# The first token tile and its gains in column halves, and all bias lines ahead of the second tile's transposes

## The chip, the cores and the metric

The kernel runs on one core of a Trainium2 chip. What counts is the time of one execution on the device in microseconds; the kernel before takes 1675.51 us (median of 3 runs, 1674.7 to 1675.98).

## The reference

One layer of a bidirectional encoder, on a prompt of 256 tokens and a sample of 1024 tokens, 1024 wide, all in float32. What matters here is its beginning:

```python
def _rmsnorm(x, g):
    x32 = x.astype(jnp.float32)
    y = x32 * lax.rsqrt(jnp.mean(x32 * x32, axis=-1, keepdims=True) + RMS_EPS)
    return (y * g.astype(jnp.float32)).astype(x.dtype)
...
    h = _rmsnorm(x, g_mix)
    z = h @ w_in
...
    rel = np.arange(3 * n)[None, :] - n - np.arange(n)[:, None]
    bias = bias_table.astype(jnp.float32)[_rel_bucket(rel * dist_scale)]
```

Tokens are normalized and scaled by the gains g, and projected to queries, keys, values and gates. Two branches of banded attention follow (one with a sink, one dilated in three groups), both with a bias that depends only on the distance of query and key, looked up in a table of 32 buckets. The branches are gated, merged and projected; an MLP with a squared ReLU and a last normalization end the layer.

## The kernel before

The 1280 tokens are ten tiles of 128 rows. A float32 product is made of three products of a high and a low part (`hi`, `lo`): ScalarE rounds to `hi`, VectorE subtracts to get `lo`, TensorE multiplies hi*hi, hi*lo and lo*hi. The order of the work in this first part is the order in which the code is written: each engine runs its instructions in that order.

The part around the change is the start (lines 689 to 908). SyncE issues the loads in program order: the first token tile (`load_x(0)`, line 702, 512 KB), the gains g spread over 128 partitions (line 831, 512 KB), the second token tile, the first half of a table `hot` (line 740, 132 KB), the first quarter of the value weights (`load_v`, line 709, 512 KB), the second half of `hot`, the other quarters, and then further token tiles and the rest. A DMA issue also waits for the landing of the DMA that stands eight before it, as they share eight semaphores in turn. The transfer of the bucket table `tab` (line 734, 2.5 KB) goes through ScalarE's queue.

Meanwhile TensorE runs `warm(15)`: 15 matmuls of the identity, whose result nobody uses (two records each in the trace). Then come the token tiles:

- `square(t)`: ScalarE squares the tile with an accumulator along the row (line 757) and takes the root of mean + eps (line 759).
- `scale(t)`: VectorE takes the reciprocal (line 763) and multiplies the tile by it and by g in one instruction (line 764), into `xn`.
- `turn(t)` is a generator of three steps: TensorE transposes `xn` in eight blocks of 128 columns into two banks of PSUM, four to a bank (line 336); ScalarE evicts four high parts (line 790) and VectorE four low parts (line 792); at last ScalarE copies plain parts for later use.
- `draw(j)`: one of four matmuls that turn the bucket table into the bias lines of all heads (line 744); j 0 and 1 read the first half of `hot`, 2 and 3 the second. All four sum into one bank, and `store_lines` reads it only during the fourth token tile.
- `split_v(0, i)`: the value weights' high part on ScalarE and low part on VectorE or GpSimd (lines 720 and 721).
- `values(t, v, ps)`: the value projection, three matmuls for each of eight blocks (line 819).

TensorE's order is: warm matmuls, transposes of tile 0, draws 0 and 1, transposes of tile 1, draws 2 and 3, value matmuls of tiles 0 and 1. ScalarE and VectorE square and scale tile 1 ahead of evicting the transposes of tile 0.

Of the kernel before, what the change touches and what calls it, by code (L numbers as in the profile page):

```python
# [10 lines left out]
F32 = mybir.dt.float32  # L11
F32R = mybir.dt.float32r
AF = mybir.ActivationFunctionType
ALU = mybir.AluOpType

P = 128
D = 1024
# [9 lines left out]
EPS = 1e-6  # L27
# [70 lines left out]
def encoder_kernel(  # L98
# [5 lines left out]
    nc = tc.nc  # L104
    PSUM = bass.MemoryType.PSUM

    def x_rows(t):
        return x_sample[0, P * t : P * (t + 1), :] if t < 8 else x_prompt[0, P * (t - 8) : P * (t - 7), :]
# [13 lines left out]
    small = ctx.enter_context(tc.tile_pool(name="small", bufs=4))  # L122
# [4 lines left out]
    def slot(name, shape=(P, D), dt=F32):  # L127
        return slots.tile(list(shape), dt, name=name, tag="m", bufs=N_M)
# [7 lines left out]
    def bank(tag, name=None):  # L136
        return psum.tile([P, 512], F32, name=name or tag, tag=tag, bufs={"mm": 3, "sc": 2, "pt": 2, "pv": 1}[tag])
# [120 lines left out]
    def copy(out, in_, scale=None):  # L258
        flip[0] ^= 1
        if flip[0]:  # L260
            nc.scalar.activation(out, in_, AF.Copy, scale=1.0 if scale is None else scale)
        elif scale is None:
            nc.vector.tensor_copy(out, in_)
        else:
            nc.vector.tensor_scalar(out, in_, scale, None, op0=ALU.mult)
# [41 lines left out]
    hp, xn = {}, {}  # L307
# [381 lines left out]
    with ExitStack() as pre:  # L689
# [5 lines left out]
        xs, sds = {}, {}  # L695
        gm = slot("gm")
        NV = (512, 384)
        v_raw, v_parts = {}, {}

        def load_x(t):  # L700
            xs[t] = slot("xt")
            nc.sync.dma_start(xs[t], x_rows(t))

        def load_v(v, i):

            raw = v_raw[v, i] = slot("vraw", (P, 2, NV[v]))
            ks = slice(2 * i, 2 * i + 2)
            if v == 0:
                nc.sync.dma_start(raw, w_in3[:, ks, OFF_V : OFF_V + 512])
            else:  # L710
                nc.sync.dma_start(raw[:, :, :P], w_in3[:, ks, 640 : 640 + P])
                nc.sync.dma_start(raw[:, :, P:], w_in3[:, ks, OFF_V + 512 : OFF_V + 768])

        def split_v(v, i, eng=nc.vector):
            if v == 0:
                hi, lo = wslot("vhi", (P, 2, 512), F32R), wslot("vlo", (P, 2, 512), F32R)
            else:
                hi, lo = own("v2", (P, 2, 384), F32R, 8), own("v2", (P, 2, 384), F32R, 8)
            src = v_raw.pop((v, i))
            nc.scalar.activation(hi, src, AF.Copy)  # L720
            eng.tensor_tensor(lo, src, hi.bitcast(F32), op=ALU.subtract)
            v_parts[v, i] = hi, lo

        def warm(n):
            ps = bank("mm", "warm")
            for _ in range(n):
                nc.tensor.matmul(ps[:, :P], ident, ident, start=True, stop=True, skip_group_check=True)

        pads = NL // 512
# [8 lines left out]
        def load_hot(i):  # L738
            hots.append(slot("hot")[: BUCKETS + 1, :])
            nc.sync.dma_start(hots[i], hot[:, D * i : D * i + D])  # L740

        def draw(j):

            nc.tensor.matmul(drawn, tab[:, edge - 32 * j : edge - 32 * j + P],
                             hots[j // 2][:, 512 * (j % 2) : 512 * (j % 2) + 512], start=not j, stop=j == pads - 1)
# [8 lines left out]
        def square(t):  # L754
            xn[t] = slot("xn")
            ss = small.tile([P, 1], F32, name="ss")
            nc.scalar.activation(xn[t], xs[t], AF.Square, accum_out=ss)
            sds[t] = small.tile([P, 1], F32, name="sd")
            nc.scalar.activation(sds[t], ss, AF.Sqrt, bias=eps, scale=1.0 / D)

        def scale(t):
            rs = small.tile([P, 1], F32, name="rs")
            nc.vector.reciprocal(rs, sds.pop(t))
            nc.vector.scalar_tensor_tensor(xn[t], xs.pop(t), rs, gm, op0=ALU.mult, op1=ALU.mult)

        def two(name):
            return [slot(name, (P, 2, 512)) for _ in range(2)]
# [53 lines left out]
        def evac(t, v, ps):  # L821
# [6 lines left out]
            nc.gpsimd.dma_start(scr_v[rows, 512 * v : 512 * v + NV[v]], vo)  # L828

        load_x(0)  # L830
        nc.sync.dma_start(gm, g_mix[0].partition_broadcast(P))
        load_x(1)
        load_hot(0)
        load_v(0, 0)
        load_hot(1)
        for i in range(1, 4):
            load_v(0, i)
        for t in range(2, 6):
            load_x(t)
# [9 lines left out]
        load_x(9)  # L849
        first = small.tile([P, 1], F32, name="sd")  # L850
        nc.scalar.activation(first, eps, AF.Sqrt)
        warm(15)

        turns = [turn(t) for t in range(NT)]
        square(0)
        scale(0)
        next(turns[0])
        draw(0)
        draw(1)
        square(1)  # L860
        scale(1)
        next(turns[0])
        split_v(0, 0)
        next(turns[1])
        draw(2)
        draw(3)
        split_v(0, 1)
        next(turns[1])
        split_v(0, 2, nc.gpsimd)
# [63 lines left out]
    if True:  # L933
# [68 lines left out]
        class Gate:  # L1002


            scale = 1.0
# [138 lines left out]
    if True:  # L1144
# [8 lines left out]
        for t in range(NT):  # L1153
            s0, m = (0, 8) if t < 8 else (8, 2)
# [215 lines left out]
    if True:  # L1370
# [140 lines left out]
        for i, (x, b, c) in enumerate(jobs):  # L1511
# [21 lines left out]
            m, sg = mT.at(c, t0, n), sgs.pop(i)  # L1533
# [74 lines left out]
    with ExitStack() as pre:  # L1608
# [7 lines left out]
        gm = slot("gm2")  # L1616
        nc.sync.dma_start(gm, g_mlp[0].partition_broadcast(P))
        xn = {}
# [10 lines left out]
        for hh in range(2):  # L1629
# [17 lines left out]
            for t in range(NT):  # L1647
                m = parts.pop(t)
# [15 lines left out]
                ss = small.tile([P, 1], F32, name="ss")  # L1664
                nc.scalar.activation(xn[t], x2[t], AF.Square, accum_out=ss)
                sd = small.tile([P, 1], F32, name="sd")
# [4 lines left out]
                rs = small.tile([P, 1], F32, name="rs")  # L1671
# [371 lines left out]
```

## Time and profile before

| | |
|---|---|
| median of 3 runs | 1675.51 us (1674.7 to 1675.98) |
| span of the profiled execution, first to last instruction | 1672.7 us |
| TensorE matmuls busy | 1661.8 us, 99% of the span |
| VectorE, ScalarE, GpSimd busy | 57%, 43%, 30% |
| first value matmul starts | 14.19 us after the span's start |
| granted TensorE clock, mean | 1.000 |

The profile gives the profiled execution by its span alone; the time of a run also holds what lies before the first and after the last instruction. Times in the trace are counted from the span's start. PE is TensorE's matmuls and PEld its weight loads, DVE is VectorE, ACT is ScalarE, POOL is GpSimd, SP is SyncE, and a q behind a name is that engine's sequencer, which issues DMAs and waits. In a row of the timeline stand start, length, engine, line, operation, result<-operands, shapes and count, and in brackets the idle time before it and what ended that.

### The profile page before, as it was taken

The page shows a single profiled execution, that of the slowest core. Times are in us where ns is not written, and L with a number is a line of the kernel's source. Part 1 is how long each engine was busy: PE and PEld are TensorE (multiplying, and loading weights), DVE is VectorE, ACT ScalarE, POOL GpSimd, SP SyncE. Part 2 cuts the span into 40 slices and gives each one's busy share as a digit, 9 for nine tenths or more (in the row PEclk, how much of TensorE's full clock was granted, in tenths as well). Part 3 has the DMA queues.
Part 4 walks back from the last instruction along what each step waited for, and adds up shares of the span by engine and source line. Part 5 has one row for each costly group of instructions (what it writes and reads, how often), then busy time and mean ns, then how long its engine had stood idle before and what let it go on. Part 6 is the DMA issues. An engine that isn't in the chain of part 4 may idle for free.

```text
span 1672.7 us, 24767 instructions
## 1 busy us (share of the span) xinstructions
PE 1661.8 (99%) x9256; PEld 1413.9 (85%) x9256; DVE 951.1 (57%) x1534; ACT 714.3 (43%) x1473; POOL 494.3 (30%) x372
## 2 busy tenths in 40 slices
PE   9999999999999999999999999999999999999998
PEld 7898888888888888888888888888888888888886
DVE  6732233455654565667278545445456775867665
ACT  6232323345654655654176333333334333333435
POOL 1212222111112352100100656455554250514240
PEclk9999999999999999999999999999999999999999
DMA  7416552666667794845121443343356934733333
GB/s 256 150 54 126 134 132 75 165 196 189 198 184 228 192 236 134 284 135 193 38 89 59 161 160 120 121 161 125 116 191 230 362 113 137 253 104 107 120 120 126
DMA packets 224176, 262.45 MB, mean 157 GB/s; under 512 B 29486, under 2 KB 153694, under 8 KB 224056
## 3 DMA queue, kind: packets, MB, share of 16 engines
q1 hardware_dynamic: 217000, 242.69, 45.4%
q0 software_dynamic: 6720, 17.65, 5.1%
q8 instruction: 73, 1.20, 0.3%
q10 hardware_dynamic: 336, 0.53, 0.1%
q14 instruction: 47, 0.39, 0.1%
HBM read 175.13 MB, written 90.92 MB: 159 GB/s over the span
## 4 chain that ended last, share of the span: by engine, by line
PE 96%; ACT 2%; DVE 1%; DMA 1%; issue 0%; SPq 0%; DVEq 0%; ACTq 0%
PE dn L345 22%; PE x L345 19%; PE mm L192 14%; PE z L345 10%; PE v L819 6%; PE y L345 5%; PE mm L345 5%; PE pv L345 3%; PE sc L345 3%; PE pt L1193 2%; PE pv L1209 2%; PE sc L553 1%; PE pv L600 1%; PE pt L586 1%; PE tr L336 1%; PE sc L1167 1%
## 5 line engine op out<-in xcount | busy, mean ns | idle before, releaser
L345 PE MATMUL dn<-dhi,ulo 128*128 128x512 f32 x448 | 174.3, 389 | 0.0
L345 PE MATMUL dn<-dlo,uhi 128*128 128x512 f32 x448 | 174.3, 389 | 0.0
L345 PE MATMUL dn<-dhi,uhi 128*128 128x512 f32 x448 | 174.3, 389 | 0.0
L345 PE MATMUL x<-chi,wlo 128*128 128x512 f32 x424 | 166.5, 393 | 0.0
L345 PE MATMUL x<-clo,whi 128*128 128x512 f32 x424 | 165.6, 390 | 0.0
L345 PE MATMUL x<-chi,whi 128*128 128x512 f32 x424 | 165.0, 389 | 0.0
L312 DVE TENSOR_TENSOR wlo<-ta,whi 128x1024 fp32r<-128x1024 f32 x30 | 56.3, 1876 | 174.0 <-ACT whi L310 174.0
L312 DVE TENSOR_TENSOR wlo<-raw,whi 128x1024 fp32r<-128x1024 f32 x60 | 89.6, 1494 | 103.1 <-ACT whi L310 98.2
L391 POOL TENSOR_TENSOR tb<-raw 128x512 f32<-128x512 f32 x25 | 32.3, 1290 | 363.7 <-DMA raw<-in_w_in_dram 111.8
L345 PEld LDWEIGHTS dn<-dhi,ulo 128*128 128x128 f32 x448 | 84.1, 188 | 17.6
L345 PEld LDWEIGHTS dn<-dhi,uhi 128*128 128x128 f32 x448 | 84.1, 188 | 17.4
L345 PEld LDWEIGHTS dn<-dlo,uhi 128*128 128x128 f32 x448 | 84.1, 188 | 17.4
L345 PEld LDWEIGHTS x<-chi,whi 128*128 128x128 f32 x424 | 79.6, 188 | 17.1
L345 PEld LDWEIGHTS x<-chi,wlo 128*128 128x128 f32 x424 | 79.8, 188 | 15.1
L345 PEld LDWEIGHTS x<-clo,whi 128*128 128x128 f32 x424 | 79.8, 188 | 14.6
L1735 POOL TENSOR_TENSOR t<-raw,t 128x1024 f32<-128x1024 f32 x16 | 46.4, 2924 | 149.2 <-DMA raw<-in_w_down_dram 149.2
L186 DVE TENSOR_TENSOR ulo<-uraw,uhi 128x1024 fp32r<-128x1024 f32 x56 | 86.1, 1558 | 4.4 <-ACT uhi L185 4.4
L1886 DVE TENSOR_TENSOR v<-v,dn 128x512 f32<-128x512 f32 x90 | 59.7, 683 | 42.3 <-PE dn L345 42.3
L186 DVE TENSOR_TENSOR dlo<-raw,dhi 128x1024 fp32r<-128x1024 f32 x32 | 50.1, 1590 | 46.3 <-ACT dhi L185 45.3
L1986 POOL TENSOR_TENSOR u<-u,u 128x640 f32<-128x640 f32 x16 | 25.1, 1569 | 173.3 <-ACT u L1904 173.3
L345 PE MATMUL dn<-dhi,up 128*128 128x512 f32 x224 | 73.5, 389 | 0.0
L345 PE MATMUL z<-chi,wlo 128*128 128x512 f32 x184 | 71.6, 389 | 0.0
(319 smaller groups left out, 4619.2 us busy)
## 6 DMA issues: line engine op xcount, KB each, us to landing
scr_u<-u SPq DMA_DIRECT2D x112, 320.0 KB, 2.6
uraw<-scr_u SPq DMA_DIRECT2D x56, 512.0 KB, 3.9
raw<-in_w_down_dram SPq DMA_DIRECT2D x36, 512.0 KB, 6.7
raw<-in_w_up_dram SPq DMA_DIRECT2D x32, 512.0 KB, 5.2
raw<-in_w_in_dram SPq DMA_DIRECT2D x25, 512.0 KB, 5.2
sg<-scr_g SPq DMA_DIRECT2D x32, 256.0 KB, 6.2
uraw<-scr_u SPq DMA_DIRECT2D x28, 256.0 KB, 4.5
qk<-scr_kb SPq DMA_DIRECT2D x48, 128.0 KB, 2.6
```

What stands on the lines that cost most here:

```text
L186: nc.vector.tensor_tensor(lo, src, hi.bitcast(F32), op=ALU.subtract)
L192: nc.tensor.matmul(ps, a, b, start=i == 0, stop=i == len(seq) - 1)
L312: nc.vector.tensor_tensor(lo, src, hi.bitcast(F32), op=ALU.subtract)
L336: nc.tensor.transpose(ps[:, P * i : P * (i + 1)], xn[t][:, P * k : P * (k + 1)], ident)
L345: nc.tensor.matmul(ps, a, b, start=first and i == 0, stop=last and i == len(seq) - 1, skip_group_check=True)
L391: (nc.vector if vector else nc.gpsimd).tensor_tensor(o, x, y, op=ALU.subtract)
L819: nc.tensor.matmul(ps[:, :n], a, b, start=k == 0 and j == 0, stop=k == KC - 1 and j == 2)
L1193: nc.tensor.transpose(ps[:, P * k : P * k + P], s[:, h, P * b : P * b + P], ident)
L1209: nc.tensor.matmul(pv[HALVES[h], P * i : P * i + P], src, pt[:, at + 2 * b + h, :], start=b == 0, stop=b == W // P - 1, skip_group_check=True)
L1735: nc.gpsimd.tensor_tensor(o, a, b, op=ALU.subtract)
L1886: nc.vector.tensor_tensor(v, v, ps, op=ALU.add)
L1986: nc.gpsimd.tensor_tensor(u[S1], u21, u22, op=ALU.add)
```

## The change

The first token tile is loaded, squared and scaled in two halves of 512 columns, and g is loaded in two halves too. The squares of the two halves go to two columns of a small tile; VectorE scales the first sum and adds eps while the second is made, and the root takes that as its bias. TensorE's transposes and the evictions of the tile are the same instructions as before. The second half of `hot` is issued ahead of the first quarter of the value weights. All four draws stand between the transposes of tile 0 and those of tile 1, and the evictions of tile 0 stand ahead of the squaring and scaling of tile 1. The warm matmuls are 13 and not 15.

```diff
+        ENDS = (slice(0, 512), slice(512, D))
+
         def load_x(t):
             xs[t] = slot("xt")
-            nc.sync.dma_start(xs[t], x_rows(t))
+            for c in ENDS if t == 0 else (slice(0, D),):
+                nc.sync.dma_start(xs[t][:, c], x_rows(t)[:, c])
...
         def scale(t):
             rs = small.tile([P, 1], F32, name="rs")
             nc.vector.reciprocal(rs, sds.pop(t))
-            nc.vector.scalar_tensor_tensor(xn[t], xs.pop(t), rs, gm, op0=ALU.mult, op1=ALU.mult)
+            x = xs.pop(t)
+            for c in ENDS if t == 0 else (slice(0, D),):
+                nc.vector.scalar_tensor_tensor(xn[t][:, c], x[:, c], rs, gm[:, c], op0=ALU.mult, op1=ALU.mult)
+
+        def square_ends():
+
+            xn[0] = slot("xn")
+            ss = small.tile([P, 2], F32, name="ss2", tag="m")
+            for i, c in enumerate(ENDS):
+                nc.scalar.activation(xn[0][:, c], xs[0][:, c], AF.Square, accum_out=ss[:, i : i + 1])
+            nc.vector.tensor_scalar(ss[:, 0:1], ss[:, 0:1], 1.0 / D, EPS, op0=ALU.mult, op1=ALU.add)
+            sds[0] = small.tile([P, 1], F32, name="sd")
+            nc.scalar.activation(sds[0], ss[:, 1:2], AF.Sqrt, bias=ss[:, 0:1], scale=1.0 / D)
...
         load_x(0)
-        nc.sync.dma_start(gm, g_mix[0].partition_broadcast(P))
+        for c in ENDS:
+            nc.sync.dma_start(gm[:, c], g_mix[0][c].partition_broadcast(P))
         load_x(1)
         load_hot(0)
+        load_hot(1)
         load_v(0, 0)
-        load_hot(1)
...
-        warm(15)
+        warm(13)
 
         turns = [turn(t) for t in range(NT)]
-        square(0)
+        square_ends()
         scale(0)
         next(turns[0])
-        draw(0)
-        draw(1)
+        for j in range(pads):
+            draw(j)
+        next(turns[0])
         square(1)
         scale(1)
-        next(turns[0])
         split_v(0, 0)
         next(turns[1])
-        draw(2)
-        draw(3)
         split_v(0, 1)
         next(turns[1])
```

## The prediction

> **What bounds the kernel now.** I read the page first: its span and the busy shares.
>
> ```profile
> span 1672.7 us, 24767 instructions
> PE 1661.8 (99%) x9256; PEld 1413.9 (85%) x9256; DVE 951.1 (57%) x1534; ACT 714.3 (43%) x1473; POOL 494.3 (30%) x372
> ```
>
> TensorE is busy for all but 10.9 us, so a change at the start can only win idle time of PE at the start, and what it wins there is kept if every later wait is counted from PE's own work. Second, the chain of waits in the first 16 us (start, length, what):
>
> ```profile
> 0.75 0.39 SPq L702
> ...
> 1.67 6.52 DMA xt<-in_x_sample_dram
> ...
> 11.26 1.09 PE tr L336 x8
> 12.35 1.91 PE line L744 x4
> 14.26 1.83 PE v L819 x7
> ```
>
> The second token tile lands at 8.2, is squared and scaled, is transposed at 11.26, two draws follow, and from 14.2 PE runs the value matmuls without a gap. Third, the busy time of each engine between those points (from:to, length, busy PE, PEld, DVE, ACT, POOL, granted clock, DMA share, GB/s):
>
> ```profile
> 6.87:8.06 1.19, 0.00 (x1) 0.00 (x1) 1.13 (x1) 0.00 (x0) 0.00 (x0) 1.00 1.01 320
> 8.06:9.08 1.02, 1.02 (x8) 0.85 (x8) 0.00 (x0) 0.87 (x1) 0.00 (x0) 1.00 1.03 301
> 9.08:11.06 1.98, 1.98 (x5) 0.67 (x4) 1.31 (x2) 1.95 (x8) 0.00 (x0) 1.00 1.05 302
> 11.06:11.26 0.20, 0.00 (x1) 0.00 (x1) 0.20 (x2) 0.20 (x1) 0.00 (x0) 1.00 1.04 389
> 11.26:12.28 1.02, 1.02 (x8) 0.85 (x8) 1.02 (x4) 0.46 (x1) 0.00 (x0) 1.00 1.05 388
> 12.28:14.19 1.91, 1.91 (x5) 0.67 (x4) 1.91 (x3) 1.88 (x5) 0.00 (x0) 1.00 1.06 395
> ```
>
> PE's work from the end of the warm matmuls to the values is 5.93 us (8 transposes 1.02, two draws 1.98, 8 transposes 1.02, two draws 1.91), with idle of 1.19 and 0.20 us. That idle, 1.39 us, and the two warm matmuls are all there is to win.
>
> **The first tile in halves.** Now (timeline: start, length): the tile lands at 4.37, but the scaling waits for the gains:
>
> ```profile
> 4.37 1.06 ACT L757 ACTIVATE xn<-xt 128x1024 f32<-128x1024 f32 x1 [1.28 <-DMA xt<-in_x_sample_dram]
> 5.56 0.30 ACT L759 ACTIVATE sd<-ss,eps 128x1 f32<-128x1 f32 x1
> 5.88 0.16 DVE L763 RECIPROCAL rs<-sd 128x1 f32<-128x1 f32 x1 [4.62 <-ACT sd L759]
> 6.72 1.28 DVE L764 SCALAR_TENSOR_TENSOR xn<-xt,rs,gm 128x1024 f32<-128x1024 f32 x1 [0.67 <-DMA gm<-in_g_mix_dram]
> ```
>
> The second half of the tile lands last, at about 4.4. Its square is bounded by half and the whole of 1.06; a line through the evictions below (4 of 256 columns in 1.18, 0.30 each) and 1.08 for 1024 columns gives 0.56. With the accumulator read, the root (0.30) and the reciprocal (0.16), 1/rms is there near 5.5. The added DVE step on the first sum lies beside the second square; uncovered it costs about as much as the reciprocal, 0.16. None of it decides, with 1 us to spare: the second half of g lands where the whole does now, and ended DVE's wait before 6.72, so the last scaling starts at 6.72 as now. It is half as wide: between 0.64 (half of 1.28) and 1.28, and I take 0.70, from the copy of that shape.
>
> ```profile
> 9.59 1.18 ACT L790 ACTIVATE hhi<-tr 128x256 fp32r<-128x256 f32 x4
> ```
> ```profile
> L825 DVE COPY vo<-v 128x512 f32<-128x512 f32 x2 | 1.4, 688 | 0.4 <-PE v L819 0.4
> ```
>
> The second four transposes then run from 7.47 to 7.99 (half of 1.02); the first four lie before. So the tile is transposed 1.09 us sooner (9.08 less 7.99).
>
> **What takes that gain.** The next PE work is the first draw, and its operand is late: the sequencer of the weight loads waits right behind the transposes (line 744), and the issue of a later x tile, which waits for the first table's landing, goes out at 8.93.
>
> ```profile
> L744 PEldq EVENT_SEMAPHORE  x1: 51/51/51, 8.9 to 8.9; - x1
> ```
> ```profile
> 8.93 0.33 SPq L702 DMA_DIRECT2D xt<-in_x_sample_dram  x1
> ```
> ```profile
> SPq L702 <- DMA hot<-in_hot_dram: 0.4, 1, 0.4
> ```
>
> The draw at 9.08 thus starts 0.15 after the landing; transposes and table come together now by chance. In the changed kernel the same bytes stand ahead of the table (first tile, g, second tile), so it still lands at about 8.93, and PE stands idle from 7.99 to 9.08. The halves win nothing there.
>
> **All draws first.** From 9.08: two pairs of 1.91 and 1.02 for the transposes, 13.92 against 14.19, a win of 0.27. That is the low end, as the second pair pays its filling again. At the high end the weight loads of the draws are one every 0.43 (12.82 and 13.25 below): 8 of them are 3.44, the values start at 9.08 + 3.44 + 1.02 = 13.54, a win of 0.65. I take 0.46. The second table, which moves ahead of the first value weights, must land by 10.8 to 11.0; now, behind 512 KB of them, it lands at 11.17 (line 840 below, which waits for it), and without these it follows the first one, which took 0.74 after the second tile (8.93 less 8.19): about 9.7.
>
> ```profile
> 12.82 0.19 PEld L744 LDWEIGHTS line<-hot,tab 33*128 33x128 f32 x1 [0.24 <-issue]
> 13.25 0.19 PEld L744 LDWEIGHTS line<-hot,tab 33*128 33x128 f32 x1 [0.24 <-issue]
> ```
>
> **The second tile** now stands behind the first one's four hi evictions on ScalarE: they end 0.59 (half of 1.18) after 8.1, at 8.7. Then the durations of the first tile above: from the start of the square to that of the root 1.19 (5.56 less 4.37), 0.30, 0.16, 1.28 and handovers of 0.15 make xn ready at 11.8. It was 11.2 (transposes from 11.26), so this is 0.6 later, but PE draws until 12.5 to 12.9; cover 0.7. Without that cover (draws ready at once) it would be the bound.
>
> **DMA queue.** Two more transfers go out, 0.4 us of SyncE each, and the first value weights are issued behind the second table. Every issue waits for the one eight before it: in these rows of SyncE's waits the ninth (line 709) waits for the first tile, line 840 for the second table, and in the row above an x tile for the first table.
>
> ```profile
> SPq L709 <- DMA xt<-in_x_sample_dram: 0.4, 1, 0.4
> SPq L840 <- DMA hot<-in_hot_dram: 0.6, 1, 0.6
> ```
> ```profile
> 10.65 1.08 ACT L720 ACTIVATE vhi<-vraw 128x1024 fp32r<-128x1024 f32 x1
> 11.17 0.38 SPq L840 DMA_DIRECT2D bg<-in_b_gate_dram  x1
> 12.31 1.06 ACT L720 ACTIVATE vhi<-vraw 128x1024 fp32r<-128x1024 f32 x1 [0.59 <-DMA vraw<-in_w_in_dram]
> 12.45 2.35 DVE L721 TENSOR_TENSOR vlo<-vraw,vhi 128x1024 fp32r<-128x1024 f32 x2
> ```
>
> The first value weights become the ninth, so they go out at about 4.4, later than now; their bytes are due at 10.65 and the queue ahead of them is full till then. They land at most where the second table lands now, 11.17: split by 12.3 (1.08) and 13.5 (1.22, half of 2.35), needed by the second value matmul at 13.9. The second weights stay at 12.31, their low part is done by 14.8 and needed at 15.2 (six matmuls later). Rows of 2 KB in place of 4 KB: the stretch of value weights (2 KB) against that of x tiles (4 KB):
>
> ```profile
> 12.30:15.00 2.70, 2.70 (x8) 1.32 (x8) 2.70 (x4) 2.69 (x6) 0.00 (x0) 1.00 1.05 398
> 15.00:17.50 2.50, 2.50 (x12) 2.06 (x11) 2.24 (x5) 2.47 (x5) 2.01 (x1) 1.00 1.02 408
> ```
>
> That is 2.5%, on 1 MB of about 2.6 us: 0.07 later.
>
> **Sum.** 0.46 less 0.07 is 0.4 us off. The profiled execution has a span of 1672.7; the median of the runs, 1675.51, is 2.8 above it, and that lies around the span and isn't touched. 1675.51 less 0.4 is 1675.1. Later nothing takes it back: PE's one large wait behind the start (1 us, ahead of 695) hangs on a chain that begins with SyncE's issue at 684.52, and that issue is released by PE's own matmuls:
>
> ```profile
> 683.11 1.40 PE mm L192 x6
> 684.52 0.00 SPq L1481
> ```
>
> **The rivals.** *The table is early* (its landing pulled ahead by smaller transfers in front): the draws start at 7.99, end at 11.4, and xn at 11.8 is the bound; values at 11.85 + 1.02 = 12.87, 1.32 sooner, 1674.2. Against it: the bytes are the same.
>
> *The table is late*, and this one comes out slower: g is one row read for 128 partitions, and its stretch moves fewer bytes than the next one:
>
> ```profile
> 4.37:6.60 2.23, 2.23 (x18) 2.23 (x17) 0.16 (x1) 1.45 (x3) 0.00 (x0) 1.00 0.93 285
> 6.60:8.20 1.60, 0.41 (x4) 0.22 (x3) 1.28 (x1) 0.00 (x0) 0.00 (x0) 1.00 1.03 333
> ```
>
> If a read of a half row costs as much as one of a whole row, g takes up to 2.23 longer, and everything in the queue behind it, second tile and tables, is as much later. PE waits for the table at line 744; from a delay of 0.46 on the change loses, at most 2.23 less 0.46, 1.8: 1677.3. Against it: rows of 2 KB from different places cost 2.5% here, as worked out above, not a doubling; for rows read from one place no run shows it.
>
> *Each transfer holds the queue for itself.* The first tile takes 3.6 us from its issue to its landing (0.75 to 4.37); its 512 KB at 398 GB/s are 1.3, so 2.3 is not bytes. Paid in series for two more transfers, that brings the table 4.6 later and the end 4.1 (4.6 less 0.46): 1679.6. Against it: the first table lands 0.74 behind the second tile, so 2.3 isn't paid between neighbours. The Trainium skill (DMA: Bandwidth & Descriptors, Anatomy of one DMA) has about 2.0 us fixed for each transfer, for the completion above all; an estimate by that in series is 4.0 us, near this price. By the row of the table the trace doesn't agree that it adds up.
>
> *The clock falls.* In the warm stretch PE's records come 17 in 3.70 us, later 13 in 1.37:
>
> ```profile
> 1.30:5.00 3.70, 3.63 (x17) 3.63 (x18) 1.00 0.81 242
> 5.50:6.87 1.37, 1.37 (x13) 1.18 (x11) 1.00 0.96 365
> ```
>
> So PE starts at half its pace for some 3.8 us, though the granted clock is 1.00 in both. With 13 matmuls the warming ends at 6.4 (4 records of 0.11 fewer than now, 6.87) and, but for the transposes, PE does nothing until 9.08: 2.7 us. If that slows it again for 3.8 us, 1.9 is lost: 1677.0. Before, this stretch was 2.2 without harm. The Trainium skill (TensorE: Matmul & The Clock Gate, Part 1 and Part 4) has an idle window of about 3.4 us and transposes that don't count as work; by it the clock holds unless the table is 0.75 late as well.
>
> *Nothing is left*: a later wait counted from the start of the program takes the 0.4: 1675.5. The chain shows none.
>
> That the transposes don't start by halves is no case of its own: all eight would end at 8.5, still before the table.
>
> **Chances.** Forecast 0.56 (1674.9 to 1675.3; with the runs' own spread, 1674.7 to 1676.0, some 1674.1 to 1676.0), table early 0.10, table late 0.18, queue held 0.02, clock 0.04, nothing left 0.10. The range runs from 1673.6 (table early, less the spread) to 1677.0 (most of table late and the clock). A measurement here can't tell less than about 0.2%, 3.4 us, from no change; the idle to be won is 1.4 and a late table costs at most 1.8, so within 0.2% has 0.95, slower 0.03 (queue held, or late and clock together), faster 0.02 (none of these cases, what I overlook).
>
> **What would show it.** Right: line 744 starts near 9.1 with PE idle before it from 8.0; eight draw records without a gap; second transposes at 12.5 to 12.9, the first value matmul at 13.5 to 13.9. Wrong: the table lands after 9.5, or the second transposes wait on DVE's scaling, or the first value matmul waits on ScalarE's split; a gain or loss of over 1.8 us would mean that something behind 25 us moved, which I don't see.

## The result and the profile after

The changed kernel takes 1682.72 us (median of 5 runs, 1681.13 to 1683.29), the kernel before in the same call 1675.29 (1674.70 to 1675.98). The ratio is 1.0043, with a 95% interval of 1.0031 to 1.0056: 7.4 us slower, where 0.4 us faster was predicted. Single executions of some kernels below fall into two groups, as the clock of TensorE fell at the start or did not.

The page of the changed kernel, its span, busy shares and granted clock:

```profile
span 1681.1 us, 24768 instructions
...
PE 1666.8 (99%) x9252; PEld 1416.6 (84%) x9252; DVE 954.3 (57%) x1536; ACT 715.2 (43%) x1475; POOL 494.7 (29%) x372
...
PEclk8999999999999999999999999999999999999999
```

The span is 8.4 us longer (1672.7 before), and PE is busy for 5.0 us more with no more work: it worked more slowly somewhere. The first of the 40 slices has a granted clock below 9 tenths. The timeline of PE and VectorE there (start, length, engine, line; in brackets the idle time before and what ended it):

```profile
7.73 0.75 DVE L769 SCALAR_TENSOR_TENSOR xn<-xt,rs,gm 128x512 f32<-128x512 f32 x1 [2.25 <-DMA gm<-in_g_mix_dram]
...
8.53 0.66 PE L336 MATMUL tr<-ident,xn 128*128 128x128 f32 x4 [2.59 <-DVE xn L769]
...
9.49 0.66 PE L336 MATMUL tr<-ident,xn 128*128 128x128 f32 x4 [0.30 <-DVE xn L769]
...
12.10 7.16 PE L747 MATMUL line<-hot,tab 33*128 33x512 f32 x8 [1.96 <-DMA hot<-in_hot_dram]
...
19.20 1.97 PE L336 MATMUL tr<-ident,xn 128*128 128x128 f32 x8
...
20.82 0.78 PE L834 MATMUL v<-vhi,hhi 128*128 128x512 f32 x1
```

Two things went another way than the prediction. The loads are late: the first table, which ended PE's wait before 12.10, landed at 11.97 (8.91 before), the second tile at 11.18 (8.19), the halves of g at 7.59 and 8.59 (whole at 6.58). And from there everything on PE is slow: eight draws in 7.16 us, eight transposes in 1.97 where they took 1.09. Cut into stretches of 3.41 us that begin where the clock changes (from:to, length, busy PE, PEld, DVE, ACT, POOL, granted clock, DMA share, GB/s):

```profile
4.34:7.76 3.42, 1.60 (x14) 1.41 (x13) 0.27 (x3) 0.91 (x3) 0.00 (x0) 1.00 0.80 223
7.76:11.17 3.41, 1.31 (x8) 0.84 (x8) 2.52 (x5) 1.32 (x4) 0.00 (x0) 1.00 1.05 238
11.17:14.58 3.41, 2.48 (x3) 1.16 (x4) 1.90 (x4) 2.06 (x4) 0.00 (x0) 0.50 1.04 352
14.58:17.99 3.41, 3.41 (x5) 1.32 (x4) 2.45 (x2) 1.50 (x2) 0.00 (x0) 0.50 1.04 402
17.99:21.41 3.42, 3.42 (x12) 2.12 (x11) 0.37 (x2) 0.87 (x3) 0.00 (x0) 0.50 1.02 347
21.41:24.82 3.41, 3.41 (x10) 2.65 (x9) 2.17 (x5) 3.38 (x6) 1.93 (x1) 0.50 0.41 50
24.82:28.23 3.41, 3.41 (x16) 2.82 (x15) 3.34 (x5) 2.72 (x8) 0.46 (x1) 1.00 0.89 256
```

The clock is at half from 11.17 to 24.82, 13.65 us. The first value matmul starts at 20.82 instead of 14.19, 6.6 later, and the values run at half pace for 4.0 us more, which loses 2.0: 8.6 together, against 8.4 in the span. At full pace the draws would have taken 3.7 (as in `order_alone` below), the transposes 1.0, and the values would have begun at about 16.8. So some 2.6 us are late loads, less what the order wins, and some 6.0 are the clock (estimates from these rows). Both had to be explained: what makes the loads late, and why the clock falls and stays down so long.

### The profile page after: what moved, and what is told of

Read it like the earlier page. It is cut to its first block, busy times and chain, and to the rows that moved or that the text cites. A ratio compares the mean times of both kernels' runs of the same rounds, so it can differ in the third digit from the quotient of the medians.

```text
span 1681.1 us, 24768 instructions
## 1 busy us (share of the span) xinstructions
PE 1666.8 (99%) x9252; PEld 1416.6 (84%) x9252; DVE 954.3 (57%) x1536; ACT 715.2 (43%) x1475; POOL 494.7 (29%) x372
## 4 chain that ended last, share of the span: by engine, by line
PE 96%; ACT 1%; DVE 1%; DMA 1%; SPq 0%; issue 0%; DVEq 0%; ACTq 0%
PE dn L345 22%; PE x L345 19%; PE mm L192 14%; PE z L345 10%; PE v L834 6%; PE y L345 5%; PE mm L345 5%; PE sc L345 3%; PE pv L345 3%; PE pt L1207 2%; PE pv L1223 2%; PE sc L553 1%; PE pv L600 1%; PE pt L586 1%; PE tr L336 1%; PE sc L1181 1%
## 5 line engine op out<-in xcount | busy, mean ns | idle before, releaser
L345 PE MATMUL z<-clo,whi 128*128 128x512 f32 x184 | 71.7, 389 | 0.0
```

The lines of the kernel that those rows point to most:

```text
L345: nc.tensor.matmul(ps, a, b, start=first and i == 0, stop=last and i == len(seq) - 1, skip_group_check=True)
```

## The experiments

Each kernel is the changed one ("after") or the one before with the edit shown; a few combine edits, as said there. "Value" is the start of the first value matmul (14.19 before, 20.82 after); all landings and starts are those of the profiled execution.

### Which part of the change does it

`order_alone`: the kernel before, with only the order of the draws, evictions and `hot` changed.

```diff
+        load_hot(1)
         load_v(0, 0)
-        load_hot(1)
...
-        draw(0)
-        draw(1)
+        for j in range(pads):
+            draw(j)
+        next(turns[0])
         square(1)
         scale(1)
-        next(turns[0])
...
-        draw(2)
-        draw(3)
```

> The kernel before with only the order of the work changed: the second table ahead of the value weights, all draws ahead of the second tile's transposes, evictions of the first tile ahead of the second tile's square; nothing in halves, 15 warm matmuls. The prediction's step: draws from 9.1 to 12.5 to 12.9, first value matmul at 13.5 to 13.9, 0.3 to 0.6 faster, 1674.7 to 1675.2, clock 1.00. Rival: the two tables in a row delay each other or the second tile, or the clock falls: 1676 or more.

Measured 1675.32 (1673.60 to 1676.52), ratio 0.9997 [0.9986, 1.0008]. The tables land at 8.61 and 9.27, the values start at 13.97. So the order alone neither delays the loads nor costs anything.

`g_halves_alone`: the kernel before, with g loaded in two halves.

```diff
-        nc.sync.dma_start(gm, g_mix[0].partition_broadcast(P))
+        for c in (slice(0, 512), slice(512, D)):
+            nc.sync.dma_start(gm[:, c], g_mix[0][c].partition_broadcast(P))
```

> The kernel before with only g in two transfers. Theory A: the second half of g lands at 8 to 8.8, the second tile at 10.5 to 11.5, the first table after 11.5 (before: 6.6, 8.2, 8.9); PE is idle for long, so the clock may fall too: 3 us slower without and some 8 us slower with it, 1678 to 1684. Theories B and C: the first table lands by 9.5, time within 1 us of before.

Measured 1681.49 (1674.24 to 1686.06), ratio 1.0020 [1.0001, 1.0040]: four of ten executions at 1674 to 1676 with a mean clock of 0.999 or 1.000, six at 1680 to 1686 with 0.994 to 0.996. In the profiled one, of the second group, the second half of g lands at 8.83 and the first table at 10.82, and the clock is at half from 11.59 to 25.24.

`g_whole`: after, with g in one transfer again.

```diff
-        for c in ENDS:
-            nc.sync.dma_start(gm[:, c], g_mix[0][c].partition_broadcast(P))
+        nc.sync.dma_start(gm, g_mix[0].partition_broadcast(P))
```

> The changed kernel with g in one transfer again. Theory A (half rows of g, read from one place for all partitions, hold up the queue, and the late tables let the clock fall): the first table lands near 9.2 as before the change, line 747 starts at 9.1 to 9.4, the granted clock stays 1.00 from about 5 us on, the first value matmul at 13.5 to 14.0, time 1674.7 to 1676. Theory B (the smaller and more numerous transfers as such, the halves of x too): the table still lands after 11, time over 1680. Theory C (13 warm matmuls and all draws in a row let the clock fall whatever the loads do): the table lands near 9.2 but the clock falls, time 1677 to 1680.

Measured 1682.24 (1681.35 to 1682.98), ratio 1.0038 [1.0028, 1.0048]: no better than after. g, now whole, lands at 8.60, the first table at 11.95. My first theory, that the two half rows of g are the price, fell.

`x_halves_alone`: the kernel before, with only the first token tile loaded in two halves; it is squared and scaled whole.

```diff
-            nc.sync.dma_start(xs[t], x_rows(t))
+            for c in (slice(0, 512), slice(512, D)) if t == 0 else (slice(0, D),):
+                nc.sync.dma_start(xs[t][:, c], x_rows(t)[:, c])
```

> The kernel before with only the first token tile loaded in two transfers, squared and scaled whole; g in one. Theory D: g lands near 8.6 and not 6.6, as in the kernel with g whole; the clock falls in most executions; median 1680 to 1683. If it takes both halves or the new order to do it: g lands by 7, 1674.5 to 1676.

Measured 1684.67 (1683.16 to 1686.61), ratio 1.0052 [1.0034, 1.0071]. This one edit is worth the whole loss: g, untouched, lands at 9.21, the second tile at 10.76, the first table at 11.43, and the clock is at half from 11.43 to 25.09. As it has 15 warm matmuls, the two that the change leaves out aren't needed for the fall. The scaling rows of the three kernels `x_halves_alone`, `g_halves_alone` and `g_whole`, each waiting for g (6.72 before):

```profile
9.34 1.28 DVE L765 SCALAR_TENSOR_TENSOR xn<-xt,rs,gm 128x1024 f32<-128x1024 f32 x1 [3.26 <-DMA gm<-in_g_mix_dram]
```
```profile
8.96 1.28 DVE L764 SCALAR_TENSOR_TENSOR xn<-xt,rs,gm 128x1024 f32<-128x1024 f32 x1 [2.58 <-DMA gm<-in_g_mix_dram]
```
```profile
8.74 1.42 DVE L769 SCALAR_TENSOR_TENSOR xn<-xt,rs,gm 128x512 f32<-128x512 f32 x2 [3.28 <-DMA gm<-in_g_mix_dram]
```

A split of either load makes g 2.0 to 2.6 late, and for g both splits together cost no more than one. That isn't all that makes the table of after 3.06 late: its second tile lands 2.59 behind g (11.18 less 8.59) where it took 1.61 before and 1.55 in `x_halves_alone`. Windows of after, about the end of the first tile and in the second tile's stretch (the last two columns are the DMA engines' busy share and GB/s):

```profile
3.50:4.30 0.80, 0.80 (x6) 0.80 (x5) 0.04 (x1) 0.80 (x3) 0.00 (x0) 1.00 0.57 138
4.30:6.00 1.70, 1.64 (x14) 1.45 (x13) 0.27 (x2) 0.95 (x3) 0.00 (x0) 1.00 0.77 130
...
8.60:11.20 2.60, 1.24 (x8) 0.77 (x8) 1.84 (x4) 1.32 (x5) 0.00 (x0) 0.99 1.03 219
```

In the last one the engines are busy throughout but move 219 GB/s, where the prediction's row of this stretch before has 333. `g_whole` shows it too (11.19 less 8.60); which part of the edits brings it, no run settles.

### What the clock counts

`warm_32`: after, with 32 warm matmuls in place of 13, which go on until 10.6.

```diff
-        warm(13)
+        warm(32)
```

> The changed kernel with 32 warm matmuls, so that PE works until about 10.2 and the tables are as late as in the changed kernel (12.1). It parts the delay from the clock. If the clock falls for lack of work between 6 and 12: it stays 1.00 here, eight draw records take 3.5 and not 7.2, the first value matmul starts at 16.6 and not 20.8, time 1677 to 1678.5; then about 2.4 of the 7.4 us are the delay and 5 to 6 the clock. If the clock falls because draws and transposes don't count as work, whatever comes before: it falls here as well, one window of 3.4 us later at most, time 1680 to 1683.

Measured 1679.56 (1677.27 to 1682.97), ratio 1.0021 [1.0009, 1.0032], value 16.95. The table is as late (11.64); keeping PE busy ahead of it takes back 2.9 us (4.5 above the kernel before measured beside it, after 7.4). But the clock still falls, behind a window in which PE was busy throughout, with draws:

```profile
12.05:15.46 3.41, 3.41 (x9) 1.21 (x8) 2.88 (x7) 3.05 (x6) 0.00 (x0) 1.00 1.05 383
15.46:18.87 3.41, 3.41 (x13) 3.03 (x14) 3.32 (x6) 2.82 (x7) 0.00 (x0) 0.50 1.04 408
```

The same is seen in `order_alone`, behind 2.83 us of draws in this window:

```profile
9.83:13.25 3.42, 3.31 (x11) 1.42 (x10) 2.89 (x6) 3.23 (x6) 0.00 (x0) 1.00 1.06 392
13.25:16.66 3.41, 3.41 (x12) 2.85 (x11) 3.06 (x6) 2.96 (x6) 0.62 (x1) 0.50 1.03 409
```

Two windows of draws in after (11.17 to 17.99, 2.48 us and 3.41 us of draws) did not bring the clock back. A draw has 33 contraction rows of 128 (its operands fill 33 of 128 partitions). If the clock follows the rows that a matmul fills, a window of draws is worth a quarter of one.

`draws_128`: after, with `tab` and `hot` zero-filled to 128 partitions, so that each draw is as long but has 128 rows.

```diff
-        tab = own("tab", (P, edge + P))[: BUCKETS + 1, :]
+        tab = own("tab", (P, edge + P))
...
-            hots.append(slot("hot")[: BUCKETS + 1, :])
-            nc.sync.dma_start(hots[i], hot[:, D * i : D * i + D])
+            hots.append(slot("hot"))
+            (nc.vector, nc.gpsimd)[i].memset(hots[i], 0.0)
+            nc.sync.dma_start(hots[i][: BUCKETS + 1, :], hot[:, D * i : D * i + D])
```

> The changed kernel with the operands of the draws filled up with zeros from 33 to 128 partitions: same bits in the result, same time per draw, but all rows of the array have operands. In the changed kernel the clock stayed at a half through two whole windows of 3.4 us full of draws (11.2 to 18.0) and came back only behind a window full of value matmuls (24.8). If work on 33 of 128 rows counts too little for the clock: here it comes back at 14.6 or 18.0, time 1678 to 1680. If draws count like the others: it stays low until about 24.8, time 1681 to 1684.

Measured 1679.52 (1677.06 to 1681.61), ratio 1.0025 [1.0015, 1.0035], value 18.36. The clock still falls ahead of the late table (11.81), but one window full of the wider draws brings it back:

```profile
5.97:9.38 3.41, 1.40 (x11) 0.97 (x9) 1.06 (x3) 0.46 (x3) 0.00 (x0) 1.00 0.91 284
9.38:12.79 3.41, 1.96 (x5) 1.22 (x6) 2.03 (x5) 1.89 (x6) 0.00 (x0) 0.50 1.04 281
12.79:16.21 3.42, 3.42 (x5) 1.35 (x4) 2.67 (x3) 2.46 (x5) 0.00 (x0) 0.50 1.05 395
16.21:19.62 3.41, 3.41 (x18) 2.36 (x17) 1.95 (x4) 1.47 (x6) 0.00 (x0) 1.00 1.03 406
```

`warm_32_draws_128`: both edits.

> The changed kernel with 32 warm matmuls and with the draws' operands filled up to 128 partitions with zeros, so that no window of the clock is without full work while the loads are as late as in the changed kernel. Theory: of the 7.4 us of the change only the delay of the loads is left. The clock stays 1.00 from about 5 us on, the tables land near 12, the first value matmul at 16.5 to 17, 1677 to 1678. Rival, the clock falls for another reason (bursts, transposes): it falls for one window or more here as well, 1679 to 1682.

Measured 1677.43 (1676.65 to 1679.74), ratio 1.0014 [1.0005, 1.0022], and the mean clock is 0.999 or 1.000 in all ten executions. In the windows that hold the draws it stays at full:

```profile
10.84:14.26 3.42, 3.42 (x21) 2.47 (x20) 1.42 (x4) 2.13 (x6) 0.00 (x0) 1.00 1.04 360
14.26:17.67 3.41, 3.11 (x14) 1.68 (x14) 2.91 (x4) 3.01 (x8) 0.00 (x0) 1.00 1.04 404
```

What is left, 2.6 us over the kernel before (1674.83, measured beside it), is delay alone: the table landed at 11.18 here, and the warm matmuls, which in this execution went on until 11.65, were a part of it. So of after's 7.4 us over the kernel before about 2.9 go back with PE kept busy ahead of the table, 1.9 more with the wider draws, and 2.6 are delay.

`order_warm_20` and `order_128`: the order alone with 20 warm matmuls, and the same with draws of 128 rows.

```diff
-        warm(15)
+        warm(20)
```

> The order alone, with 20 warm matmuls that fill PE until 8.0, when the first transposes can start. If the executions of the kernel before at 1678 to 1681 (5 of 31) are ones in which the clock fell for want of work ahead of 8.0: none over 1677 here, and the single window at half clock that the order alone showed (13.2 to 16.7) is gone; 1674 to 1675. If warm matmuls ahead of 8.0 don't bear on it: as the order alone, 1675.3, with a window at half clock in most.

> The order alone with 20 warm matmuls and draws on 128 partitions, all transfers whole: the part of the change that the prediction counted on, without what costs the clock. Theory: no window at half clock in any execution, first value matmul at 13.5 to 13.9, 0.5 to 1 us faster than before, 1674.0 to 1674.6. Rival: the win stays below what can be seen, 1675.

`order_warm_20` measured 1675.35 (1673.06 to 1675.87), ratio 0.9996 [0.9987, 1.0006], value 13.81. `order_128` measured 1674.17 (1673.53 to 1675.70, 12 executions) against 1674.83, ratio 0.9992 [0.9984, 1.0001]; all twelve have a mean clock of 0.999, `order_warm_20` has that in two of ten and 0.997 or 0.998 in the others (one window at half is 0.001 of the span). In the profile of `order_128` the two windows that hold the draws are at full clock, as is the next:

```profile
6.78:10.19 3.41, 3.41 (x27) 2.98 (x26) 1.58 (x3) 1.05 (x4) 0.00 (x0) 1.00 1.03 332
10.19:13.61 3.42, 3.12 (x10) 1.28 (x9) 2.89 (x7) 3.38 (x6) 0.00 (x0) 1.00 1.05 390
```

Beside the first four experiments 4 of 31 executions of the kernel before were above 1678 (the expectation has 5).

`order_128` is the best kernel of the study, 0.7 us below the one before, but the interval touches 1, so that it is faster isn't shown. Its values start at 14.13, since its transposes first wait for the warm matmuls (8.50) and then for the second tile's scaling (13.28).

`g_first`: the kernel before, with g issued ahead of the first tile, both whole.

```diff
-        load_x(0)
         nc.sync.dma_start(gm, g_mix[0].partition_broadcast(P))
+        load_x(0)
```

> The kernel before with g issued ahead of the first token tile, each in one transfer. If the one-place reads of g are slow by themselves (128 reads at 213 GB/s or less): g lands at 5 to 5.5, the first tile behind it at 6 to 6.5, the second tile at 8.2 as before, the first scaling at about 8, 1 us later than before, 1675 to 1677. If they are slow only behind another transfer whose ends put the engines out of step: g lands by 4.2, the tile by 5.7, the second tile by 7.4, 1674 to 1675.

Measured 1682.71 (1682.21 to 1684.65), ratio 1.0047 [1.0030, 1.0064]. The later loads are nearly on time (second tile 8.68, first table 8.97). Only the first tile is late (6.83), so its transposes start at 9.90 instead of 8.06. That is enough: behind this window, with 1.03 us of PE's work in it, the clock falls, from 9.68 to 26.74, and the values start at 21.11.

```profile
6.27:9.68 3.41, 1.03 (x9) 0.84 (x8) 1.28 (x2) 2.42 (x5) 0.00 (x0) 1.00 1.05 328
```

### Why the loads are late

`x_one_2k`: the kernel before, with the first tile in one transfer of 2 KB pieces (the left columns of the first two tiles, so the tile holds other numbers).

```diff
+                nc.sync.dma_start(xs[t].rearrange("p (h c) -> p h c", h=2),
+                                  x_sample[0, : 2 * P, :512].rearrange("(h p) c -> p h c", p=P))
```

> The kernel before, the first token tile still in one transfer, but of 256 pieces of 2 KB, as the value weights have them. (To get such pieces it takes the left columns of the first and of the second tile; so the first tile holds other numbers.) Theory P, pieces of 2 KB put the DMA engines out of step: g lands near 9 as with the tile in column halves (9.2), 1682 to 1686. Theory T, a transfer more ahead of g does it: g lands by 7, 1674 to 1676.

Measured 1675.72 (1675.02 to 1680.24), ratio 1.0010 [1.0001, 1.0019], two of ten executions at 1680 with a mean clock of 0.996: g 6.73, first table 9.27. Pieces of 2 KB are not the cause.

`x_row_halves`: the kernel before, with the first tile in two transfers of 64 rows, pieces of 4 KB.

```diff
+            for r in (slice(0, 64), slice(64, P)) if t == 0 else (slice(0, P),):
+                nc.sync.dma_start(xs[t][r, :], x_rows(t)[r, :])
```

> The kernel before, the first token tile in two transfers of 64 rows each, in pieces of 4 KB. Theory P: g lands by 7 as before (6.6), 1674 to 1676. Theory T: g lands near 9, 1682 to 1686.

Measured 1684.94 (1682.77 to 1688.96), ratio 1.0064 [1.0047, 1.0081]: g 9.09, first table 11.10. One more transfer does it, whatever the shape of its pieces.

`sink_between`: the kernel before, with a 4 KB transfer that it makes anyway (the sink's values) moved right behind the first tile.

```diff
         load_x(0)
+        nc.sync.dma_start(nsink, sink[0].partition_broadcast(P))
         nc.sync.dma_start(gm, g_mix[0].partition_broadcast(P))
...
-        nc.sync.dma_start(nsink, sink[0].partition_broadcast(P))
```

> The kernel before, the first token tile in one transfer; the issue of the 4 KB of sinks (32 bytes for each partition) is moved from later to between the tile and g. Theory T in the form that g's later issue does it (0.47 us later than before, with the first tile drained meanwhile): g lands near 9, 1682 to 1686. Theory P, or T in the form that it takes a large transfer more: g lands by 7.1, 1674 to 1676.

Measured 1683.70 (1683.11 to 1684.54), ratio 1.0054 [1.0039, 1.0069]: g 8.48, second tile 10.15, first table 10.85. So 4 KB between tile and g cost 8.7 us in the end. Windows of 1 us, of the kernel before, then `x_halves_alone`, then `sink_between`:

```profile
3.50:4.50 1.00, 1.00 (x6) 1.00 (x6) 0.00 (x0) 0.13 (x1) 0.00 (x0) 1.00 0.85 230
4.50:5.50 1.00, 1.00 (x8) 1.00 (x7) 0.00 (x0) 1.00 (x2) 0.00 (x0) 1.00 0.93 229
```
```profile
3.50:4.50 1.00, 1.00 (x6) 1.00 (x6) 0.00 (x0) 0.10 (x1) 0.00 (x0) 1.00 0.56 141
4.50:5.50 1.00, 1.00 (x11) 1.00 (x10) 0.00 (x0) 1.00 (x2) 0.00 (x0) 1.00 0.65 156
```
```profile
3.50:4.50 1.00, 1.00 (x6) 1.00 (x6) 0.00 (x0) 0.11 (x1) 0.00 (x0) 1.00 0.21 62
4.50:5.50 1.00, 1.00 (x7) 1.00 (x6) 0.00 (x0) 1.00 (x2) 0.00 (x0) 1.00 0.45 177
```

The DMA engines stand idle about the first tile's end: in these 2 us, on the mean of the 16 engines, for 0.22 us before (0.15 and 0.07), 0.79 with the halves, 1.34 with the 4 KB. So a part of the delay can be time in which little is moved. Idle time alone doesn't make loads late, though: in `g_third` below the engines are busy for 0.73 and 0.75 of the time from 4.5 to 6.5, and its loads are on time.

The traces show more. The landing of each of these large loads is recorded in 16 steps, and the load counts as landed at the last. First and last step, in us:

| load | before | `x_halves_alone` | `sink_between` |
|---|---|---|---|
| g | 5.81 to 6.58 | 5.75 to 9.21 | 5.83 to 8.48 |
| second tile | 7.15 to 8.19 | 7.62 to 10.76 | 7.55 to 10.15 |

The first parts of g are as early as before; only the last ones are late. In `x_half_act` below, 15 steps of g stand by 5.87 and the last comes at 8.20. That each step is one DMA engine's share, and that some engines fall behind and hold up what is queued on them, would fit; the traces don't name the engine of a step.

`g_rows`: after, with the halves of g read from 128 different rows (other data, so the gains are left out); `x_halves_g_rows`: `x_halves_alone` with g's place filled so in one transfer.

```diff
-            nc.sync.dma_start(gm[:, c], g_mix[0][c].partition_broadcast(P))
+            nc.sync.dma_start(gm[:, c], x_prompt[0, :P, c])
```

> The changed kernel, but the two transfers into g's place read 128 different rows of the prompt and not one row 128 times; bytes, sizes and order of the transfers are the same. Left out: the gains g (the tokens are scaled by other numbers). Theory D (128 reads of one place are slow as soon as the DMA engines don't run in step, and halves of either transfer put them out of step): the second half lands by 6.2, the second tile by 8.2, the first table by 9.2 (changed kernel: 8.6, 11.2, 12.0), the clock stays, 1674.5 to 1676. Theory B (more and smaller transfers as such): lands as late as in the changed kernel, over 1680.

> The kernel with only the first tile in halves (g landed at 9.2), but g's one transfer reads 128 different rows of the prompt. Left out: the gains g. If the slow third transfer is slow because its 128 reads go to one place: g's place is filled by 5.8, the second tile lands by 7.5, the table by 8.5, 1674 to 1676. If any third transfer is slow here: filled at 8 or later, over 1680.

`g_rows` measured 1678.66 (1675.44 to 1681.79), ratio 1.0019 [1.0007, 1.0030]: the halves land at 5.34 and 6.99, but the second tile still at 9.80 and the first table at 10.74. `x_halves_g_rows` measured 1681.98 (1674.39 to 1684.83, two of ten executions without a fall of the clock), ratio 1.0032 [1.0018, 1.0046]: g's place is filled at 8.76, the first table lands at 11.36. That g is one row read for all partitions is a part of the delay with two halves of it, not the cause.

`g_third`: the kernel before, with g behind the second tile, all three whole.

```diff
-        nc.sync.dma_start(gm, g_mix[0].partition_broadcast(P))
         load_x(1)
+        nc.sync.dma_start(gm, g_mix[0].partition_broadcast(P))
```

> The kernel before with g issued behind the second tile (third, as in the slow kernels), all transfers whole. If one-place reads are slow in the third place or at a later issue as such: the second tile lands near 5.7, g at 9.5 or later, its stretch 4 us long, the tables after 10. If they are slow only where the transfer ahead of them is a small or half one: g takes its 2.2 us and lands near 8.0, the tables at 8.9 as before. The first scaling is late in both, so that the clock falls in both; the landings decide, not the time (1680 to 1686).

Measured 1682.76 (1679.83 to 1685.01), ratio 1.0039 [1.0026, 1.0051]: second tile 5.52, g 8.02, first table 8.62. The third of three large transfers isn't late as such; the loss goes with the later first scaling (transposes from 9.49) and the clock, at half from 12.19 to 22.43.

`x_halves_tab_later`: `x_halves_alone` with ScalarE's small transfer of `tab` moved to SyncE behind the second tile; `x_half_act`: `x_halves_alone` with the tile's second half issued by ScalarE.

```diff
-        nc.scalar.dma_start(tab[:BUCKETS, edge : edge + NH], rel_bias)
...
         load_x(1)
+        nc.sync.dma_start(tab[:BUCKETS, edge : edge + NH], rel_bias)
```
```diff
+                (nc.scalar if c.start else nc.sync).dma_start(xs[t][:, c], x_rows(t)[:, c])
```

> The kernel with only the first tile in halves; the 2.5 KB of the bucket table go out on SyncE's queue behind the second tile, so that nothing is issued by ScalarE. If that small transfer on the other queue takes the DMA engines from the third transfer: the engines don't run dry near 3.5 us, g lands by 7.1, 1674 to 1676. If the third transfer is late by itself: g lands near 9 as before this edit, over 1680.

> The kernel with only the first tile in halves, the second half issued by ScalarE (behind the bucket table), so that g is the second transfer of SyncE's queue again. If being third in SyncE's queue behind 512 KB makes g late: g lands by 7.1, 1674 to 1676. If it is the number of transfers on all queues: near 9, over 1680.

They measured 1684.04 (1681.04 to 1685.10), ratio 1.0051 [1.0036, 1.0066], and 1684.43 (1683.76 to 1685.68), ratio 1.0055 [1.0038, 1.0072]. Without ScalarE's transfer g lands at 7.70, the first table at 10.56: 1.5 of g's delay of 2.6 goes, and 0.9 of the table's 2.5. Such differences are to be read with care: the four traces with the loads of after (after, `draws_128`, `warm_32`, `warm_32_draws_128`) have the second half of g at 8.20 to 9.14 and the first table at 11.18 to 11.97. With the second half on ScalarE's queue g, second on SyncE's, lands at 8.20, and the first square waits until 8.52. So the small transfer may be a part of the cause, but neither it nor the place in SyncE's queue is the whole. Why parts of the loads come late when one more transfer stands at the start stays open.

## Why the prediction was wrong, point by point

**"In the changed kernel the same bytes stand ahead of the table (first tile, g, second tile), so it still lands at about 8.93."** This step failed first: it landed at 11.97. The same bytes didn't land at the same time: one more transfer ahead of g is enough to bring the last parts of g, and of all behind it, some 2 to 2.6 us late (`sink_between`, `x_halves_alone`). In after the table was later still, with the DMA engines of after busy for 0.57 and 0.77 of the time about the first tile's end, and its second tile moved at 219 GB/s where the kernel before moved 333. The rival *the table is late* (0.18) had the right place, but its mechanism, half rows of g as dear as whole ones, fell with `g_whole`, and its size was at most 2.23 where 3.06 was measured. *Each transfer holds the queue* (0.02) was nearer: it priced each of two more transfers at 2.3 us. One costs 1.9 to 2.6 for g, the second hardly anything more. The Trainium skill (DMA: Bandwidth & Descriptors, Anatomy of one DMA) gives a fixed cost of about 2.0 us for a transfer on GpSimd's path. The delay by one added transfer, on SyncE's path here, is of that size, but the traces don't agree that it is paid for each in series.

**The clock's rival was priced with one window.** It had 3.8 us at half pace, 1.9 lost. Measured are 13.65 us, and some 6.0 of the 8.4. The mechanism, a wait of PE ahead of the table, was right (`warm_32` takes 2.9 us back). The warming ended at 5.94, not 6.4, as full clock came at 4.34 in this trace and at 5.35 in that of the kernel before. Two things were missed: that a late table and the fall come together, which the chances had in 0.03 with "slower", and that the work behind the wait, the draws, can't bring the clock back. By the rule that the prediction drew from the Trainium skill (TensorE: Matmul & The Clock Gate, Part 1 and Part 4) the clock held unless the table was 0.75 late; it was 3.1 late, so the condition was met, and the fall agrees with it. The half of the rule on transposes doesn't hold here, as the last section shows.

**The draws as work like any other.** The sum took eight draws at full pace as cover for the second tile. In 7.16 of after's 13.65 us at half pace they were the work, and the count in the last section has them at a quarter.

**What held.** *All draws first* was to start the values at 13.5 to 13.9 without late loads: 13.97 in `order_alone`, whose transposes end at half clock, and 13.81 in `order_warm_20`; neither is measurably faster than the kernel before. *The halves win nothing*: no run shows them win, but as every run with halves of the tile has late loads, none tests it alone; in the trace of after scaling is 0.75 for a half (0.70 taken) and squaring 0.63 (0.56 taken). *Rows of 2 KB* cost little: the first tile of `x_one_2k` lands at 4.81, those of the kernel before, `order_alone`, `order_warm_20` and `order_128` at 4.35 to 4.72. *Later nothing takes it back*: PE's wait at line 192 is 0.9 us, 0.8 before, in the waits of both. The test "wrong if the table lands after 9.5" caught the case; "a loss over 1.8 means that something behind 25 us moved" did not: nothing behind 25 us moved.

**Range and chances.** 1673.6 to 1677.0 was far too narrow, since each rival was priced alone; what came, 0.43% slower, stood under a chance of 0.03. A late table with a fall of the clock was the one case that had to be priced together, since the first brings on the second.

## What to carry to other kernels

Before loads at the start are split or moved, look at how long TensorE has full-height work in each 3.4 us around them: a delay of 2 us cost 8 here, as it let the clock fall and what followed was in part matmuls with few rows. Count transfers at the start, not bytes: a half landing earlier may hold up all that is queued behind it. Where a few matmuls on few rows have to stand alone, zero-filling their rows can keep the clock (`warm_32_draws_128`).

## What the hardware showed that was not expected

**The clock counts rows.** In all 20 traces the clock changes only at multiples of 3.41 us from its first change. The Trainium skill (TensorE: Matmul & The Clock Gate, Part 1) has a free-running window of 3413 ns, and the traces agree with it. I then counted, for every window of the first 32 us, PE's busy time, times the granted clock, with the draws on 33 rows at 33/128 and all else, transposes too, in full. One bound between 1.46 and 1.51 us separates all 164 windows: 110 at or above it are followed by full clock, 54 below it by half. Any weight of the draws from 0.19 to 0.29 separates them all; counted in full, the best bound leaves 6 wrong. Those nearest to the bound, with some of the others:

| window | PE busy | of it draws on 33 rows | clock | count | next |
|---|---|---|---|---|---|
| `sink_between`, 5.58 to 9.00 | 1.40 | 0 | 1.0 | 1.40 | half |
| `draws_128`, 5.97 to 9.38 | 1.40 | 0 | 1.0 | 1.40 | half |
| `g_third`, 8.77 to 12.19 | 2.70 | 1.67 | 1.0 | 1.46 | half |
| `g_third`, 5.36 to 8.77 | 1.51 | 0 | 1.0 | 1.51 | full |
| `x_one_2k`, 10.93 to 14.34 | 3.04 | 2.02 | 1.0 | 1.54 | full |
| `order_warm_20`, 7.79 to 11.20 | 3.07 | 2.03 | 1.0 | 1.56 | full |
| `g_whole`, 18.93 to 22.34 | 3.41 | 0.32 | 0.5 | 1.59 | full |
| before, 8.76 to 12.17 | 3.21 | 1.98 | 1.0 | 1.74 | full |
| `order_alone`, 9.83 to 13.25 | 3.31 | 2.83 | 1.0 | 1.21 | half |
| `warm_32`, 12.05 to 15.46 | 3.41 | 3.39 | 1.0 | 0.89 | half |
| after, 17.99 to 21.41 | 3.42 | 1.27 | 0.5 | 1.24 | half |

The windows of `g_third` as the profile has them, and that of the kernel before:

```profile
5.36:8.77 3.41, 1.51 (x14) 1.32 (x12) 0.78 (x2) 1.73 (x6) 0.00 (x0) 1.00 0.91 299
8.77:12.19 3.42, 2.70 (x12) 1.53 (x12) 3.34 (x7) 2.00 (x5) 0.00 (x0) 1.00 1.05 341
```
```profile
8.76:12.17 3.41, 3.21 (x16) 1.68 (x14) 2.42 (x6) 2.93 (x8) 0.00 (x0) 1.00 1.05 339
```

At half clock a window that is busy throughout counts 1.71, just over the bound: to come back takes a window with almost no gap and almost no draws, which is why the fall in after lasts four windows. The rule was found in these traces after the runs, and was not tried on a run made to break it; the zero-filled draws are what was tested. The Trainium skill (TensorE: Matmul & The Clock Gate, Part 4) says of a transpose that it "doesn't count as PE-busy the same way". Here the measurement differs: left out, with the best weight for the draws and the best bound, 10 of the 164 windows come out wrong; counted in full, none.

The kernels with loads on time stand near the edge: 1.74 in the trace of the kernel before, 1.54 in `x_one_2k`. Measured beside the experiments, 6 of 107 executions of the kernel before took 1678 to 1682 us at a mean clock of 0.995 to 0.997. None of these six has a trace, so that the same count explains them is not shown.

**One small transfer at the start costs 2 us.** 4 KB between two loads of 512 KB leaves the DMA engines idle for 1.34 of 2 us on their mean and brings the next load 1.9 us later (`sink_between`, 8.48 against 6.58), though its first part lands as before (5.83 against 5.81). No run settled why.
